# Group size and buffers of the later adaLN products in a two-layer mixer kernel on Trainium2

## The chip, the cores and the metric

The kernel runs on one core of one Trainium2 chip. The metric is device time in microseconds of one execution; before the change the median of three executions is 1592.39 us (1588.01 to 1595.9). The profile shows one further execution, in which the hardware profiler recorded every instruction, every semaphore update and every DMA packet.

## What is computed

Two transformer layers run over 1024 tokens and 256 context tokens of width 1024. Both layers are modulated by a condition vector. This is the part that the change touches:

```python
def adaln_params(cond, w, b):
    m = jax.nn.silu(cond) @ w + b
    return jnp.split(m, 3, axis=-1)          # shift, scale, gate
...
for layer in range(DEPTH):                   # DEPTH = 2
    need_ctx = layer < DEPTH - 1
    shx, scx, gtx = adaln_params(c, adaln_w[layer], adaln_b[layer])
    shc, scc, gtc = adaln_params(c_ctx, adaln_w[layer], adaln_b[layer])
    hx = rms_norm(x, norm_g[layer]) * (1.0 + scx[:, None, :]) + shx[:, None, :]
    hc = rms_norm(ctx, norm_g[layer]) * (1.0 + scc) + shc
    ...                                      # layer 0: attention, layer 1: gated linear attention
    x = x + gtx[:, None, :] * (ox @ w_out[layer])
    if need_ctx:
        ctx = ctx + gtc * (oc @ w_out[layer])
```

`adaln_w` is 2 x 1024 x 3072 in float32. Layer 0's shift and scale are needed at once and are made at the start. Layer 0's gate and all of layer 1's shift, scale and gate are needed later; these are the "later products".

## The kernel before

Layer 0 projects the tokens, six units of weights one after another, and attends: heads of a windowed attention (family A) and of a differential attention (family B, four heads). Function `layer0_heads` runs steps u = 1 to 6. In each step the attention of an earlier unit (`l0_attn_a` or `l0_attn_b`) is written together with fill work for TensorE (`l0_proj`, the projection of unit u, and in step 6 `l0_gates`); `merge` draws the fill in by its costs. In step u = ADP = 4, which has the second family B head and the projection of unit 4, the fill is woven by `weave` with `adaln_later`, a piece for every 2100 units of fill.

`adaln_later` calls `adaln_rows` three times: 256 columns a row group for layer 0's gate, then twice 384 columns for layer 1. One call sums over KB = 8 contraction blocks of 128. For each block it takes two tiles `aw` (128 partitions by 2 x 256 or 2 x 384 columns) from a ring of AWB = 3 buffers, starts their loads on the queue of SyncE (line 238), and issues four matmuls (line 242). The stationary operand is the condition `s32`, 128 x 32; matmul j writes columns 32j to 32j+31 of the array and partitions 32j to 32j+31 of the PSUM tile `AD` (`tile_position`). So there are 3 x 8 x 4 = 96 matmuls and 48 loads. Each matmul is float32 and has two records in the trace. After a call VectorE adds the bias rows `arb` (line 245), and for layer 1 `adaln_cols` transposes the rows and writes `sh1` and `ga1`.

The order within each engine is not the order of the source: when the program is built, a scheduler places each instruction by its own timing and by priority, which follows the source. `ahead(kind)` raises the priority by as many places as AHEAD gives for that kind (`high_priority(offset=n)`). Each engine then runs its list in order; SyncE's queue too is served in order, so a load that waits for a buffer holds up everything behind it.

Names in the rows: `proj` (line 399) are projections, `SX` (1021) the scores of the attention, `T` transposes (`<-ident,p` line 1034, `<-identr,hb` lines 817 and 821), `O` (1046 to 1048, 1064, 1077) the attention's value products and the norms behind them, `h` tiles of normalised tokens loaded from `hT_d`, `wraw` raw weights, `oT_d` the attention's results. The tile pool of the later products, `l0d`, lives in step 4 only.

Of the kernel before, what the change touches and what calls it, by code (L numbers as in the profile page):

```python
# [19 lines left out]
P = 128  # L20
D = 1024
KB = 8
# [44 lines left out]
XP = 2  # L67
NPRE = 0
ADP = 4
AWB = 3  # L70
EPP = 5
RB = 0
PB = 0
AHEAD = dict(gate=100)

ENG = dict(raw="aaaa", vhi="avaa", hb="avaa", qe="avaa", ke="avaa", whi="aaaa", sc="aaaa", pn="pppp", vlo="vppp", wlo="vvvv", hblo="vvvv", sq="aaaa", cos="vvpp", rot="vvpp", xn="vvvv", z="vvvv", x1="vvvv", olo="vvvv")
PSA = dict(T="01", SC="@SX", proj="36", SX="245", O="7")
# [56 lines left out]
class K:  # L134
# [13 lines left out]
    def psum(self, **banks):  # L148

        self.banks = banks  # L150
        self.turn = dict.fromkeys(banks, 0)

    def ahead(self, kind):

        n = AHEAD.get(kind, 0)
        return self.tc.high_priority(offset=n) if n else nullcontext()
# [68 lines left out]
    def adaln_rows(self, layer, c0, n, stage, per, psum, out_pool):  # L225

        nc, a = self.nc, self.a
        ps = psum()
        br = self.st(out_pool, [P, n], "arb")
        for j in range(4):  # L230
            nc.sync.dma_start(br[32 * j:32 * j + 32, :],
                              a["adaln_b"][layer:layer + 1, c0 + n * j:c0 + n * (j + 1)].to_broadcast([32, n]))
        for k in range(KB):
            yield 860 * n / 512
            w = {}
            for j0 in range(0, 4, per):
                t = stage(per * n)
                nc.sync.dma_start(t, a["adaln_w"][layer, k * P:(k + 1) * P, c0 + n * j0:c0 + n * (j0 + per)])
                for j in range(per):
                    w[j0 + j] = t[:, n * j:n * j + n]  # L240
            for j in range(4):
                nc.tensor.matmul(ps[32 * j:32 * j + 32, 0:n], lhsT=self.s32[:, k, :, :].rearrange("p a b -> p (a b)"),  # L242
                                 rhs=w[j], start=(k == 0), stop=(k == KB - 1), tile_position=(0, 32 * j))
        rows = self.st(out_pool, [P, n], "ar")
        nc.vector.tensor_tensor(rows, ps[:, 0:n], br, op=ALU.add)
        return rows
# [41 lines left out]
    def adaln_later(self, pool):  # L288

        nc = self.nc  # L290
        psum = lambda: self.st(self.ps, [P, 512], "AD")
        stage = lambda n: self.st(pool, [P, 384 * APER], "aw", bufs=AWB)[:, 0:n]
        rows = yield from self.adaln_rows(0, 2048, 256, stage, APER, psum, pool)
# [1426 lines left out]
```

## Time and profile before

| | before |
|---|---|
| executions | 1595.9, 1592.39, 1588.01 us; median 1592.39 |
| profiled execution | 1597.08 us, of which its span 1595.3 us |
| TensorE busy | 1482.9 us, 93% of the span |
| VectorE, ScalarE, GpSimd busy | 1017.0, 792.4, 579.6 us (64, 50, 36%) |
| granted TensorE clock, mean | 0.974 |
| line 242, the later products | 96 matmuls, 192 records, between 528.8 and 667.9 us |

A record of a matmul starts when it reads its operands and ends (modelled) when its results are out, so successive ones overlap; the distance between the starts of successive rows is what TensorE spends. The chain of waits is followed back from the last instruction; a wait in it is shown from the start of what was waited for, so a "DMA" piece of the chain is the whole transfer, also where TensorE worked during part of it.

### The profile page before, as it was taken

What the parts mean: (1) busy time and instruction counts of PE and PEld (TensorE: products, weight loads), DVE (VectorE), ACT (ScalarE), POOL (GpSimd) and SP (SyncE); (2) the same over time, 40 slices, a digit from 0 to 9 for tenths busy, and PEclk for the clock granted to TensorE, in tenths of its full rate; (3) what the DMA queues carried; (4) which work ended last, traced back from release to release, by engine and by line L of the source; (5) the groups of instructions that cost most, each with busy time, mean ns of one, the idle gap of its engine ahead of it and who ended that gap; (6) DMA issues with size and microseconds to landing.
All of it is one profiled execution on the core that took longest, in us unless ns stands there. A gap on an engine that the chain in (4) does not pass through costs nothing.

```text
span 1595.3 us, 26832 instructions
## 1 busy us (share of the span) xinstructions
PE 1482.9 (93%) x9460; PEld 1302.5 (82%) x9460; DVE 1017.0 (64%) x2488; ACT 792.4 (50%) x2153; POOL 579.6 (36%) x857
## 2 busy tenths in 40 slices
PE   6897998999899999999999899989989999997998
PEld 4897977888798877688898777878878998896897
DVE  3787678768667666577765767638854536237565
ACT  3665667776756655466645634345642413224111
POOL 1756777988745554247100000001111212112111
PEclk9898999999999999999999999999999999999999
DMA  9732314322231565623323368655673635425542
GB/s 343 301 145 91 120 67 126 126 70 97 83 115 68 175 230 185 199 83 116 104 80 129 123 198 295 249 187 188 231 242 108 237 132 194 166 94 182 168 149 106
DMA packets 108399, 251.30 MB, mean 158 GB/s; under 512 B 10372, under 2 KB 58500, under 8 KB 94440
## 3 DMA queue, kind: packets, MB, share of 16 engines
q1 hardware_dynamic: 108264, 249.58, 46.1%
q8 instruction: 75, 1.23, 0.3%
q14 instruction: 60, 0.49, 0.1%
HBM read 196.78 MB, written 52.76 MB: 156 GB/s over the span
## 4 chain that ended last, share of the span: by engine, by line
PE 65%; DVE 8%; DMA 7%; ACT 4%; issue 3%; POOL 2%; SPq 0%; ACTq 0%; DVEq 0%; POOLq 0%
PE proj L399 40%; PE SX L1021 4%; PE T L1034 2%; PE AD L242 2%; PE S L399 1%; PE O L942 1%; DMA wraw<-in_w_out 1%; DMA wraw<-in_w_head 1%; PE T L931 1%; PE O L1048 1%; PE O L1046 1%; PE O L1047 1%; PE T L1462 1%; ACT p L993 1%; DMA h<-g_d 1%
## 5 line engine op out<-in xcount | busy, mean ns | idle before, releaser
L399 PE MATMUL proj<-w,h 128*128 128x384 f32 (+2 forms) x2544 | 555.2, 359 | 9.1 <-DVE qs L696 3.8
L399 PEld LDWEIGHTS proj<-w,h 128*128 128x128 f32 x2544 | 437.1, 192 | 49.8 <-DVE qs L696 5.4
L399 PE MATMUL proj<-h,w 128*128 128x256 f32 x1800 | 268.3, 291 | 14.0 <-DVE w L412 2.9
L399 PEld LDWEIGHTS proj<-h,w 128*128 128x128 f32 x1800 | 241.3, 194 | 27.4 <-DVE w L412 4.5
L993 ACT ACTIVATE p<-SX,bnm 128x512 f32<-128x512 f32 (+1 forms) x208 | 124.3, 610 | 52.2 <-DVE bnm L986 38.0
L1444 POOL TENSOR_SCALAR Ts<-U,alpha 128x256 f32<-128x256 f32 x64 | 36.9, 577 | 244.4 <-DVE U L1440 244.4
L913 POOL TENSOR_TENSOR wt<-praw,wt 128x512 fp32r<-128x512 f32 (+1 forms) x96 | 114.8, 1209 | 25.5 <-ACT wt L912 20.6
L1021 PE MATMUL SX<-k,q 128*128 128x512 f32 (+1 forms) x416 | 109.0, 371 | 3.4 <-ACT p L993 3.3
L981 DVE TENSOR_REDUCE bnm<-SX 128x1 f32<-128x512 f32 x128 | 86.2, 685 | 39.9 <-PE SX L1021 39.2
L223 POOL TENSOR_TENSOR qr<-qss,mhalf 128x4 f32<-128x4 f32 (+1 forms) x60 | 65.6, 1094 | 67.5 <-DVE qss L769 62.7
L1021 PEld LDWEIGHTS SX<-k,q 128*128 128x128 f32 x416 | 69.0, 190 | 19.8 <-ACT p L993 7.1
L1440 DVE SCALAR_TENSOR_TENSOR U<-U,alpha,S 128x256 f32<-128x256 f32 x64 | 30.6, 478 | 81.4 <-PE S L399 65.1
L787 POOL TENSOR_TENSOR qs<-qs,tab 128x64 f32<-128x64 f32 (+1 forms) x192 | 73.0, 406 | 11.2 <-DVE qs L776 3.3
L223 POOL TENSOR_TENSOR brr<-brs,mhalf 128x2 f32<-128x2 f32 x20 | 16.6, 831 | 164.3 <-DVE brs L1067 145.2
L414 ACT CAST wt<-T 128x512 fp32r<-128x512 f32 (+1 forms) x104 | 50.8, 511 | 43.9 <-PE T L1034 43.6
L415 DVE TENSOR_TENSOR wt<-T,wt 128x512 fp32r<-128x512 f32 (+1 forms) x104 | 59.1, 580 | 13.6 <-ACT wt L414 13.2
L911 ACT COPY praw<-T 128x512 f32<-128x512 f32 (+1 forms) x96 | 49.6, 542 | 34.8 <-PE T L931 34.2
L414 ACT CAST kmt<-T 128x128 fp32r<-128x128 f32 x72 | 18.7, 266 | 95.0 <-PE S L399 48.2
L897 POOL TENSOR_SCALAR p<-p,arz 128x640 f32<-128x640 f32 (+2 forms) x80 | 59.7, 759 | 15.9 <-DVE arz L895 10.4
L223 POOL TENSOR_TENSOR nr<-nms,mhalf 128x1 f32<-128x1 f32 x20 | 11.7, 586 | 146.4 <-DVE nms L339 146.4
L399 PE MATMUL proj<-w,ohl 128*128 128x512 f32 x240 | 62.0, 402 | 2.6 <-DVE ohl L741 1.7
L414 ACT CAST w<-wraw 128x768 fp32r<-128x768 f32 (+2 forms) x48 | 33.7, 727 | 59.9 <-DMA wraw<-in_w_head 37.1
(310 smaller groups left out, 3395.4 us busy)
## 6 DMA issues: line engine op xcount, KB each, us to landing
h<-hT_d SPq DMA_DIRECT2D x50, 1024.0 KB, 5.0
h<-h_d SPq DMA_DIRECT2D x38, 1024.0 KB, 5.0
aw<-in_adaln_w SPq DMA_DIRECT2D x32, 384.0 KB, 3.8
h_d<-h SPq DMA_DIRECT2D x10, 1024.0 KB, 7.3
wraw<-in_w_head SPq DMA_DIRECT2D x24, 384.0 KB, 4.0
xin<-in_x SPq DMA_DIRECT2D x16, 512.0 KB, 5.5
hT_d<-h SPq DMA_DIRECT2D x8, 1024.0 KB, 5.5
g_d<-qs SPq DMA_DIRECT2D x40, 128.0 KB, 1.7
```

Of the source, the lines that this page charges most:

```text
L223: self.nc.gpsimd.tensor_tensor(out, x, self.mhalf[: x.shape[0], : x.shape[1]], op=ALU.pow)
L399: nc.tensor.matmul(ps, lhsT=x, rhs=y, start=(k == 0 and m == 0), stop=(k == n - 1 and m == 2))
L414: self.nc.scalar.copy(hi, src)
L415: self.nc.vector.tensor_tensor(lo, src, f(hi), op=ALU.subtract)
L787: nc.gpsimd.tensor_tensor(m[:, h0:h0 + n, 32 * s:32 * s + 32], xn[:, h0:h0 + n, 32 - 32 * s:64 - 32 * s], sv, op=ALU.mult)
L897: (nc.vector if hh < PN else nc.gpsimd).tensor_scalar(pv[:, hh], pv[:, hh], rz[:, hh:hh + 1], 0.0, op0=ALU.mult, op1=ALU.add)
L911: (nc.vector.tensor_copy if mode == 2 else nc.scalar.copy)(raw, src)
L913: (nc.vector if mode == 4 else nc.gpsimd).tensor_tensor(lo, raw, f(hi), op=ALU.subtract)
L981: nc.vector.tensor_reduce(nmx[:, s, c:c + 1], B, axis=AX.X, op=ALU.max, negate=True)
L993: nc.scalar.activation(pe[s][:, col:col + w], B, AF.Exp, bias=nm, accum_out=Z[:, s, c:c + 1])
L1021: nc.tensor.matmul(out, lhsT=q[:, 2 * x + s, :], rhs=kk[:, s, ks], start=(x == 0), stop=(x == 1))
L1444: nc.gpsimd.tensor_scalar(t, u, self.alpha[:, 4 * d + h, n:n + 1], 0.0, op0=ALU.mult, op1=ALU.add)
```

## The change

The loop over the eight contraction blocks becomes a loop over two groups of ADK = 4. In a group the eight loads come first, with the same cost yielded after each block's two loads, then the group's 16 matmuls, under `ahead("ad")` with an offset of 600. They are written in reverse, last block and last column group first, so that the first matmul of the program order needs the tile that was loaded last; the flags for starting and ending the sum go with the new order. The ring of `aw` has eight buffers, one group's.

```diff
-AWB = 3
+AWB = 8
+ADK = 4
...
-AHEAD = dict(gate=100)
+AHEAD = dict(gate=100, ad=600)
...
-        for k in range(KB):
-            yield 860 * n / 512
+        for k0 in range(0, KB, ADK):
             w = {}
-            for j0 in range(0, 4, per):
-                t = stage(per * n)
-                nc.sync.dma_start(t, a["adaln_w"][layer, k * P:(k + 1) * P, c0 + n * j0:c0 + n * (j0 + per)])
-                for j in range(per):
-                    w[j0 + j] = t[:, n * j:n * j + n]
-            for j in range(4):
-                nc.tensor.matmul(ps[32 * j:32 * j + 32, 0:n], lhsT=self.s32[:, k, :, :].rearrange("p a b -> p (a b)"),
-                                 rhs=w[j], start=(k == 0), stop=(k == KB - 1), tile_position=(0, 32 * j))
+            for k in range(k0, k0 + ADK):
+                for j0 in range(0, 4, per):
+                    t = stage(per * n)
+                    nc.sync.dma_start(t, a["adaln_w"][layer, k * P:(k + 1) * P, c0 + n * j0:c0 + n * (j0 + per)])
+                    for j in range(per):
+                        w[k, j0 + j] = t[:, n * j:n * j + n]
+                yield 860 * n / 512
+            with self.ahead("ad"):
+                for k in reversed(range(k0, k0 + ADK)):
+                    for j in reversed(range(4)):
+                        nc.tensor.matmul(ps[32 * j:32 * j + 32, 0:n],
+                                         lhsT=self.s32[:, k, :, :].rearrange("p a b -> p (a b)"), rhs=w[k, j],
+                                         start=(k == ADK - 1), stop=(k == KB - ADK), tile_position=(0, 32 * j))
```

Line 242 of before is line 246 after, and line 238 is 239; other lines behind the change move by five. In the rows of the program's order below, x2 stands for two matmuls in a row of the same operands' tiles; the numbers behind the names tell buffers apart.

TensorE's list where the later products begin, before (`AD` from line 242, two matmuls for each tile `aw`):

```order
L1021 MATMUL SX_7380<-k_5635,q_6360 128x256 x2
L242 MATMUL AD_7352<-aw_7422,s_17_124 32x256 x2
L242 MATMUL AD_7352<-aw_7424,s_17_124 32x256 x2
L242 MATMUL AD_7352<-aw_7461,s_17_124 32x256 x2
L1034 MATMUL T_7051<-ident_61,p_6735 128x128 x2
L399 MATMUL proj_7335<-w_7318,h_6511 128x384
L1021 MATMUL SX_7438<-k_5635,q_6360 128x256 x2
L399 MATMUL proj_7335<-w_7318,h_6511 128x384 x2
L399 MATMUL proj_7335<-w_7323,h_6511 128x384
L1046 MATMUL O_7095<-wt_1573_6897,v_3843 128x256
L1047 MATMUL O_7095<-wt_1573_6897,v_3843 128x256
L242 MATMUL AD_7352<-aw_7463,s_17_124 32x256 x2
```

The same place after:

```order
L1026 MATMUL SX_7384<-k_5635,q_6360 128x256 x2
L246 MATMUL AD_7352<-aw_7545,s_17_124 32x256 x2
L246 MATMUL AD_7352<-aw_7543,s_17_124 32x256 x2
L246 MATMUL AD_7352<-aw_7463,s_17_124 32x256 x2
L246 MATMUL AD_7352<-aw_7461,s_17_124 32x256 x2
L246 MATMUL AD_7352<-aw_7428,s_17_124 32x256 x2
L246 MATMUL AD_7352<-aw_7426,s_17_124 32x256 x2
L246 MATMUL AD_7352<-aw_7360,s_17_124 32x256 x2
L246 MATMUL AD_7352<-aw_7358,s_17_124 32x256 x2
L1039 MATMUL T_7051<-ident_61,p_6735 128x128 x2
L404 MATMUL proj_7335<-w_7318,h_6511 128x384
L1026 MATMUL SX_7438<-k_5635,q_6360 128x256 x2
```

A whole group stands in one piece, at the place where six matmuls stood. The second group follows 22 rows behind the first.

TensorE's fourth group after, the one with a foreign row in it (the fifth has two projections in it, behind its first two matmuls):

```order
L246 MATMUL AD_7874<-aw_8380,s_17_124 32x384 x2
L246 MATMUL AD_7874<-aw_8378,s_17_124 32x384 x2
L246 MATMUL AD_7874<-aw_8339,s_17_124 32x384 x2
L246 MATMUL AD_7874<-aw_8337,s_17_124 32x384
L1069 MATMUL O_7589<-ones_68,sc_7616 128x1 x2
L246 MATMUL AD_7874<-aw_8337,s_17_124 32x384
L246 MATMUL AD_7874<-aw_8251,s_17_124 32x384 x2
```

Here 7 and 9 matmuls stand on the two sides of a small product; of the six groups four are unbroken.

SyncE's queue at one place before, where loads of `aw`, of tokens `h` and stores of results alternate:

```order
L1081 DMA oT_d_87<-sc_7612 128x256
L358 DMA h_7835<-hT_d_80 128x2048
L238 DMA aw_8196<-in_adaln_w 128x768
L358 DMA h_8114<-hT_d_81 128x2048
L238 DMA aw_8198<-in_adaln_w 128x768
L238 DMA aw_8245<-in_adaln_w 128x768
```

SyncE's queue after, ahead of the sixth group:

```order
L1086 DMA oT_d_87<-sc_7612 128x256
L363 DMA h_7831<-hT_d_80 128x2048
L363 DMA h_8110<-hT_d_81 128x2048
L239 DMA aw_8787<-in_adaln_w 128x768
L239 DMA aw_8789<-in_adaln_w 128x768
L239 DMA aw_8791<-in_adaln_w 128x768
L239 DMA aw_8793<-in_adaln_w 128x768
L239 DMA aw_8800<-in_adaln_w 128x768
```

The eight loads of a group (five of them shown) now stand together, behind a store and two loads of `h`. The loads of the first group stand further back in the queue than the first three did (row 151 instead of 82), still far ahead of step 4.

## Rows read from the trace of the kernel before

**Rows 1.** The page: busy time by engine, chain by engine and by line.

```profile
PE 1482.9 (93%) x9460; PEld 1302.5 (82%) x9460; DVE 1017.0 (64%) x2488; ACT 792.4 (50%) x2153; POOL 579.6 (36%) x857
...
PE 65%; DVE 8%; DMA 7%; ACT 4%; issue 3%; POOL 2%; SPq 0%; ACTq 0%; DVEq 0%; POOLq 0%
```

**Rows 2.** Chain of waits, 525 to 680 us: shares, pieces (start us, us, what).

```profile
by line: PE proj L399 32.6%; PE AD L242 18.7%; PE SX L1021 14.2%; PE T L1034 7.1%; DMA aw<-in_adaln_w 5.4%; PE O L1048 4.2%; PE O L1046 3.8%; PE O L1047 3.7%; PE T L817 2.1%; PE O L1077 1.6%; PE O L1064 1.3%; PE T L821 1.1%; ACT p L993 1.0%
...
528.38 0.47 PE SX L1021 x4
...
546.86 0.44 PE T L1034 x4
...
551.57 0.92 PE SX L1021 x4
...
571.51 3.13 PE proj L399 x18
...
612.17 0.47 PE T L817 x4
...
628.91 0.34 PE O L1064 x4
```

**Rows 3.** Stretches: busy us (x) of PE, PEld, DVE, ACT, POOL; clock, DMA, GB/s.

```profile
10.00:34.00 24.00, 19.92 (x281) 13.26 (x274) 10.35 (x30) 8.41 (x18) 0.88 (x1) 1.00 1.05 400
...
528.00:668.00 140.00, 136.26 (x865) 101.49 (x863) 84.19 (x222) 75.42 (x221) 62.43 (x109) 0.99 0.61 201
```

**Rows 4.** The same columns, neighbouring stretches and the one with waits.

```profile
760.00:800.00 40.00, 36.45 (x264) 33.97 (x263) 30.30 (x75) 23.03 (x66) 5.94 (x11) 0.96 0.28 97
...
640.00:660.00 20.00, 17.24 (x99) 10.64 (x99) 9.29 (x19) 9.31 (x28) 6.68 (x12) 0.91 0.77 238
697.00:815.00 118.00, 111.76 (x772) 104.70 (x771) 86.09 (x222) 73.97 (x220) 48.14 (x79) 0.99 0.31 105
```

**Rows 5.** Line 242 alone, 515 to 680 us: busy PE and PEld, clock, DMA.

```profile
515.00:680.00 165.00, 32.76 (x192) 6.64 (x192) 0.99 0.58 191
```

**Rows 6.** TensorE in order of time: start us, us, line, form, records [idle before <-releaser].

```profile
528.78 1.06 PE L242 MATMUL AD<-aw,s 128*32 128x256 f32 x12
529.77 0.44 PE L1034 MATMUL T<-ident,p 128*128 128x128 f32 x2
...
532.38 0.63 PE L242 MATMUL AD<-aw,s 128*32 128x256 f32 x4 [0.97 <-DMA aw<-in_adaln_w]
532.93 0.51 PE L1021 MATMUL SX<-k,q 128*128 128x256 f32 x2
...
537.65 0.66 PE L1034 MATMUL T<-ident,p 128*128 128x128 f32 x4
538.23 0.63 PE L242 MATMUL AD<-aw,s 128*32 128x256 f32 x4
538.79 0.66 PE L1034 MATMUL T<-ident,p 128*128 128x128 f32 x4
539.20 0.71 PE L1021 MATMUL SX<-k,q 128*128 128x512 f32 x2
```

**Rows 7.** The same view, products with 384 columns.

```profile
577.81 1.48 PE L242 MATMUL AD<-aw,s 128*32 128x384 f32 x12
579.23 0.49 PE L1077 MATMUL O<-sc,ones 128*128 128x128 f32 x2
...
589.07 0.85 PE L242 MATMUL AD<-aw,s 128*32 128x384 f32 x8
589.85 0.39 PE L1046 MATMUL O<-wt,v 128*128 128x256 f32 x1
...
592.83 0.83 PE L242 MATMUL AD<-aw,s 128*32 128x384 f32 x2
593.59 0.44 PE L1034 MATMUL T<-ident,p 128*128 128x128 f32 x2
```

**Rows 8.** The same view, the two waits behind 645 us and what follows them.

```profile
647.55 0.84 PE L242 MATMUL AD<-aw,s 128*32 128x384 f32 x4 [1.17 <-DMA aw<-in_adaln_w]
...
651.22 1.48 PE L242 MATMUL AD<-aw,s 128*32 128x384 f32 x4 [1.60 <-DMA aw<-in_adaln_w]
652.62 1.11 PE L1034 MATMUL T<-ident,p 128*128 128x128 f32 x4
653.39 0.99 PE L399 MATMUL proj<-w,h 128*128 128x384 f32 x2
```

**Rows 9.** DMA issues: tiles, queue, count, KB each, median us to landing.

```profile
h<-hT_d SPq DMA_DIRECT2D x50, 1024.0 KB, 5.0
...
aw<-in_adaln_w SPq DMA_DIRECT2D x32, 384.0 KB, 3.8
...
aw<-in_adaln_w SPq DMA_DIRECT2D x16, 256.0 KB, 2.9
```

**Rows 10.** Line 238, all its loads: landing; SyncE's waits (total us, times, longest).

```profile
DMA to landing us min/median/max: 2.6/3.6/8.4
...
SPq L358 <- PE proj L399: 280.2, 68, 15.5
```

**Rows 11.** SyncE in order of time: three stores that end the heads of family B.

```profile
565.49 0.33 SPq L1081 DMA_DIRECT2D oT_d<-sc  x1
...
677.64 19.17 SPq L1081 DMA_DIRECT2D oT_d<-sc  x2
...
815.11 0.38 SPq L1081 DMA_DIRECT2D oT_d<-sc  x1
```

**Rows 12.** Chain of waits behind step 4: the transfers in it.

```profile
753.90 2.62 DMA wraw<-in_w_gate
...
812.82 6.21 DMA h<-hT_d
```

## The prediction

> **What bounds the kernel now.** I read the page first, for which engine sets the time. TensorE is busy for 93% of the span and makes 65% of the chain of waits; no other engine has over 8% of it [rows 1]. So what the change gives must come off TensorE, and in one stretch only, the fourth step of layer 0, where line 242 runs. The chain of that stretch is the second view: the later products are 18.7% of its 155 us, 29.0 us, and transfers of their weights another 5.4% [rows 2]. The third is the table of stretches: between 528 and 668 us TensorE is busy for 136.26 of 140 us while VectorE, ScalarE and GpSimd have 84, 75 and 62 us [rows 3]. A microsecond taken off TensorE there is therefore at first worth a microsecond; the question is what comes up behind it.
>
> **What the products cost now.** Line 242 has 192 records in 32.76 us of busy time [rows 5], in 39 separate rows of TensorE's list in order of time, of which rows 6 and 7 show five and rows 8 two. Read the distances between starts. With 256 columns, 4 records (two matmuls) hold TensorE for 532.93 - 532.38 = 0.55 us, and 12 records (six matmuls) for 0.99 us [rows 6]. With 384 columns, 2 records (a single matmul) cost 0.76 us, 8 records (four) 0.78 us, and 12 records 1.42 us [rows 7]. So one matmul costs as much as four: those on four different column groups run beside each other, as one round, and a round that holds one or two wastes the rest. A further round in the same piece adds 0.99 - 0.57 = 0.42 us (0.57 being my value for a first round with 256 columns, from 0.55) or 1.42 - 0.78 = 0.64 us. The busy time of a row reaches some 0.07 us into the next one (0.63 against 0.55), so the 39 rows hold TensorE for about 32.76 - 39 x 0.07 = 30.0 us.
>
> **What they cost in groups.** Sixteen matmuls in one piece are four rounds: 0.57 + 3 x 0.42 = 1.83 us, or 0.78 + 3 x 0.64 = 2.70 us. Two groups of the first and four of the second width make 14.5 us. The fourth and fifth group are broken once each, into 7 + 9 and 2 + 14; each break costs a round more at a first round's price, 0.78 us. That is 16.0 us: **14.0 us less**. Then the way into a piece: four transposes ahead of line 242 take 538.23 - 537.65 = 0.58 us, the same four ahead of a score product 539.20 - 538.79 = 0.41 us [rows 6]. I take 0.1 us for each entry (bounds 0 and 0.17); 8 pieces instead of 39 save **3.1 us** (0 to 5.3).
>
> **Waits of before that go.** TensorE stood for 0.97, 1.17 and 1.60 us on loads of `aw` [rows 6, 8], **3.7 us**: a load could start only when one of three buffers came free. Behind the last of these waits the granted clock fell to 0.91 in the mean of 640 to 660 us [rows 4], a few microseconds at the lower of its two levels: a round took 652.62 - 651.22 = 1.40 instead of 0.77 us, four transposes 0.77 instead of 0.41 us [rows 8, 6]. That is **1.0 us** more.
>
> **Waits that come.** The ring holds one group, so the next group's eight loads start when a burst has ended, and the next burst needs the last of them at once. TensorE's list is in order: everything behind the burst, projections, scores and transposes, waits with it. The first group has its loads long before. For the others I set the work that stands between two bursts against the loading. Prices of the work, from starts: a projection 3.13 / 18 = 0.174 us, a score product 0.23 (512 columns) or 0.12 (256), a transpose 0.11, the other kind 0.12, a product of ones 0.17 [rows 2], a value product 0.12, which I set equal to the 256-column score. Between the first and second burst stand 9 projections, 10 + 6 transposes, 2 + 4 scores, 6 value products and 2 of ones: 1.57 + 1.82 + 0.94 + 0.72 + 0.34 = 5.4 us. The same count gives 15.6, 10.4, 13.2 and 12.0 us for the four later gaps (43, 29, 48 and 24 projections among them). Loading: in the prologue, all loads back to back, the core moved 400 GB/s [rows 3], which is 0.66 us for 256 KB, 0.98 us for 384 KB, 2.6 us for a 1 MB tile `h`. With the median landing of the first, 2.9 or 3.8 us [rows 9], eight take 2.9 + 7 x 0.66 = 7.5 us (8.0 us with a `wraw` among them) or 3.8 + 7 x 0.98 = 10.7 us, and 13.3 us where an `h` is ahead. The waits are then 8.0 - 5.4 = 2.6, 0, 0.3, 0.1 and 13.3 - 12.0 = 1.3 us: **4.3 us lost**. Bounds: 0, if other engines hold up the work between the bursts and the loads get their time; and, with the longest landing seen, 8.4 us [rows 10], 8.1 + 0 + 4.9 + 2.1 + 3.3 = 18.4 us. I take 4.3, nearer to the medians. One of them, the 2.6 us, is longer than the one that brought the clock down, so **1.0 us** goes for that (0 to 4).
>
> **Idle time that comes up.** In the next step, with the same attention and projections and no later products, TensorE is busy for 111.76 of 118 us, idle for 5.3% [rows 4]; in step 4 it is never idle for another engine, because the products fill the holes. Some 100 us of other work stay there (136.26 - 32.76, less the entries). At 5.3% that is 5.3 us; where the bursts and waits let the others catch up, nothing. About 43 us of the work come behind the last burst and have no filler. I take **4.0 us** lost (0 to 8.9, the latter at the 8.9% of 760 to 800 us).
>
> **At no cost.** VectorE's bias sums, the column copies, the bias loads and the stores of the rows keep their number; they read results that come earlier than before. The first eight loads move back in SyncE's queue, past stores and two loads of `h`, to a place still far ahead of 528 us. The larger pool delays the reload of layer 0's gate rows in the queue; they are used two steps later. The scheduler's order behind step 4 shifts too; from the transfers in the chain there, 2.62 and 6.21 us long [rows 12], I allow 4 us either way.
>
> **Sum**, against the profiled execution: 14.0 + 3.1 + 3.7 + 1.0 - 4.3 - 1.0 - 4.0 = 12.5 us less than 1597.1, which is 1584.6 us. That execution lies 4.7 us above the median of the three, 1592.4; against the median the forecast is **1580 us**.
>
> **Rivals.** First, the gain is taken up by the pace of the other engines. The head's end is stored at 565.49, 677.64 + 19.17 = 696.81 and 815.11 us [rows 11]: step 4 takes 131.3 us, the next one 118.3 us. If everything but TensorE needs those 118.3 us, no more than 13 us can be had, and with TensorE idle at the 8.9% of the worst neighbour and the order behind it 1.5 us worse, 12.5 - 4.9 - 1.5 = 6 us are left: 1586 us, within what counts as no change. For it speaks that the neighbours do idle; against it that VectorE, the busiest of the others, has 73% there.
>
> Second, slower: SyncE's queue holds the loads up. Groups 3 to 6 have loads behind loads of `h`, and those wait for TensorE to leave a buffer: 280.2 us over 68 waits, 4.1 in the mean, 15.5 at most [rows 10]. If each of the four groups starts loading 6 us late, the waits are 2.6 + 3.7 + 6.3 + 6.1 + 7.3 = 26 us with 5 us at the lower clock, and 17.1 + 4.7 - 26 - 5 - 4 = -13: 1605 us. It decides from about 13 us of waiting on. Against it: before, the loads of the same `h` tiles stood ahead of loads of `aw` too, and most of these buffers come free ahead of the burst.
>
> Third, the clock. What is seen: behind the wait of 1.60 us a round ran at 1.40 us, not 0.77 [rows 8]. If every one of the five later bursts ran so, they would cost their 1.83 + 4 x 2.70 = 12.6 us again, and the time would stay at 1592 us. The Trainium skill's page "TensorE: Matmul & The Clock Gate" (Loop structure matters more than you think) names just this pattern as bad, a wait for a DMA between bursts of matmuls, after which they run cold; the trace agrees at 651 us and not at 532 us, where a wait of 0.97 us was followed by rounds at full price. Against the rival: between the bursts TensorE has 5 to 16 us of other work, and only one or two waits are as long as that.
>
> That the change doesn't do what it says can be left aside: the list of each engine is fixed, and four of six groups stand in one piece.
>
> **How the numbers follow.** 0.60 for the forecast, 0.24 for the pace of the others (1586), 0.08 for the clock (1592), 0.08 for the queue (1605). Half a per cent, 8 us, is about what a measurement tells from no change: faster 0.60, same 0.32, slower 0.08. The range runs from 1570, with the new waits and the idle time near 0 and the entries at their upper bound, to 1594, past the clock's case; it leaves out the queue's and about as much below.
>
> **What would show it.** In the profile after, line 246 should be busy for some 16 to 17 us in 8 rows, four of them with 32 records at 1.8 or 2.7 us; a wait of 2 to 4 us on `aw` ahead of the second burst, under 2 us ahead of the others; step 4, by the same stores, some 12 us shorter, the steps behind as long as before. TensorE idle for 8% or more behind the last burst would be the first rival, waits of 6 us with stalled `h` loads the second, bursts of 3.5 us and more the third. The forecast is wrong if the step gets shorter but the end does not follow.

## The result and the profile after

The changed kernel takes 1578.72 us in the median of four executions (1574.15 to 1580.66), the kernel before 1592.93 us in the median of four (1588.01 to 1595.9). The ratio is 0.9901, with a 95% interval of 0.9876 to 0.9926: 14.2 us less, where 1580 us was forecast. The profiled execution took 1577.39 us, 19.7 us less than the profiled one of before; that this difference is larger than the one of the medians comes up again below.

The page of the changed kernel: span, TensorE's busy time, and the chain by engine (compare [rows 1]).

```profile
span 1575.7 us, 26816 instructions
...
PE 1471.4 (93%) x9460; PEld 1304.4 (83%) x9460; DVE 1015.9 (64%) x2488; ACT 793.1 (50%) x2153; POOL 581.5 (37%) x857
...
PE 62%; DVE 11%; DMA 6%; ACT 4%; issue 3%; POOL 2%; SPq 0%; DVEq 0%; ACTq 0%; POOLq 0%
```

TensorE lost 11.5 us of busy time with the same number of instructions; the other engines' work is unchanged to 2 us. VectorE's share of the chain of waits rose from 8 to 11%, and TensorE's fell from 65 to 62%.

The later products, line 246, between 515 and 680 us (busy us of PE and PEld, clock, DMA; compare [rows 5]):

```profile
515.00:680.00 165.00, 17.94 (x192) 6.25 (x192) 0.97 0.52 182
```

The same 192 records are busy for 17.94 us, not 32.76. In TensorE's order of time (start us, us, line, form, records, [idle before <-releaser]) they are eight rows, of which these are the first seven, with what stands around the first two:

```profile
522.90 1.93 PE L246 MATMUL AD<-aw,s 128*32 128x256 f32 x32
524.77 0.44 PE L1039 MATMUL T<-ident,p 128*128 128x128 f32 x2
...
531.42 0.45 PE L404 MATMUL proj<-w,h 128*128 128x384 f32 x1 [1.73 <-ACT w L164]
...
533.58 3.20 PE L246 MATMUL AD<-aw,s 128*32 128x256 f32 x32
536.71 0.62 PE L404 MATMUL proj<-w,h 128*128 128x384 f32 x2
...
552.53 2.79 PE L246 MATMUL AD<-aw,s 128*32 128x384 f32 x32
...
565.90 1.49 PE L246 MATMUL AD<-aw,s 128*32 128x384 f32 x14
567.33 0.61 PE L1069 MATMUL O<-ones,sc 128*128 128x1 f32 x4
567.86 2.12 PE L246 MATMUL AD<-aw,s 128*32 128x384 f32 x18
...
583.10 0.84 PE L246 MATMUL AD<-aw,s 128*32 128x384 f32 x4
...
584.50 2.77 PE L246 MATMUL AD<-aw,s 128*32 128x384 f32 x28
```

The first burst holds TensorE for 524.77 - 522.90 = 1.87 us, the price of four rounds that the prediction gave (1.83). Three things are new. The products are over at 602 us, where before they reached 668. There is one wait of note, 1.73 us, and it isn't ahead of a burst: a projection waits for ScalarE to write a `w`, a tile of converted weights. And the second burst, 2.2 us behind that wait, takes 536.71 - 533.58 = 3.13 us where the first took 1.87; these are matmuls at the lower of the clock's two levels, 1.2 GHz, as behind the wait in [rows 8].

The table of stretches, with the columns of [rows 3]: the few microseconds around the second burst, the products' stretch, and step 4 behind the last burst.

```profile
523.00:537.00 14.00, 11.91 (x107) 8.10 (x108) 8.11 (x24) 6.06 (x18) 5.70 (x9) 0.88 0.68 214
...
523.00:602.00 79.00, 76.79 (x585) 61.66 (x585) 46.15 (x126) 42.19 (x124) 36.35 (x65) 0.98 0.79 286
602.00:682.00 80.00, 74.45 (x464) 67.02 (x461) 60.60 (x167) 51.55 (x153) 44.05 (x80) 0.96 0.25 86
```

Around the second burst the granted clock is 0.88 in the mean. In the products' stretch TensorE is idle for 2.2 us (3.7 before, [rows 3]), and behind the last burst for 5.6 of 80 us. What it waits for there, the three longest (engine, line, waited for: us, times, longest):

```profile
PE SX L1026 <- ACT p L998: 2.2, 4, 1.6
PE T L1039 <- DVE bzs L1005: 1.4, 1, 1.4
PE proj L404 <- ACT w L164: 0.8, 1, 0.8
```

The first two are the attention's own waits, for ScalarE's and VectorE's part of the softmax: the idle time that the prediction expected once no products stand in those holes. Part of it was there before: in the 29 us between the last product and the end of step 4, before, TensorE was idle for 3.1 us.

Last, the stores that end the heads of family B on SyncE's queue (compare [rows 11]):

```profile
558.97 0.33 SPq L1086 DMA_DIRECT2D oT_d<-sc  x1
...
682.00 0.32 SPq L1086 DMA_DIRECT2D oT_d<-sc  x1
...
796.19 0.32 SPq L1086 DMA_DIRECT2D oT_d<-sc  x1
```

Step 4 takes 123.0 us from start to start, the next one 114.2 us. Before, it was 131.0 and 118.6 us by the same starts (696.50 us is the start of the second store in the row that begins at 677.64; the prediction's 131.3 and 118.3 go by the end of that row). The two together are 12.4 us shorter.

### The profile page after: what moved, and what is told of

Its sections match the earlier page's. It is cut to its first block, busy times and chain, and to the rows that moved or that the text cites. A ratio compares the mean times of both kernels' runs of the same rounds, so it can differ in the third digit from the quotient of the medians.

```text
span 1575.7 us, 26816 instructions
## 1 busy us (share of the span) xinstructions
PE 1471.4 (93%) x9460; PEld 1304.4 (83%) x9460; DVE 1015.9 (64%) x2488; ACT 793.1 (50%) x2153; POOL 581.5 (37%) x857
## 4 chain that ended last, share of the span: by engine, by line
PE 62%; DVE 11%; DMA 6%; ACT 4%; issue 3%; POOL 2%; SPq 0%; DVEq 0%; ACTq 0%; POOLq 0%
PE proj L404 40%; PE SX L1026 4%; PE T L1039 2%; DMA wraw<-in_w_out 1%; PE S L404 1%; DMA h<-g_d 1%; PE O L947 1%; PE T L936 1%; ACT p L998 1%; PE AD L246 1%; DMA D<-D_d 1%; DVE bnm L986 1%; PE O L1053 1%; PE O L1052 1%; PE O L1051 1%
```

## The experiments

The theory on trial: TensorE pays for a round whether one or four matmuls are in it, and the gain comes from whole rounds. The rivals: the gain comes from the eight buffers (loads earlier, no waits on `aw`); from the longer groups; or from the products being done earlier. "Busy" below is line 246's (242's) busy time between 500 and 700 us, "hold" the sum of the distances from each of its rows to the next row, "to the end of layer 0" the time from the first product to the start of the last record of layer 0's output projection. Within that time, "idle" is TensorE's idle time, and "at 1.2 GHz" the time for which its other work, all but the products, ran at the lower of the two granted clocks. Pieces are counted in the program's order of TensorE. Ratios are to the kernel before on the same chip.

| kernel | pieces | busy us | hold us | idle us | at 1.2 GHz, us | to the end of layer 0, us | median us | ratio (95%) |
|---|---|---|---|---|---|---|---|---|
| before | 39 | 32.76 | 30.0 | 26.5 | 15.1 | 508.2 | 1592.93 | |
| before_again | 39 | 32.78 | 30.0 | 25.2 | 15.3 | 506.6 | 1594.9 (one) | |
| changed | 8 | 17.94 | 17.4 | 22.8 | 21.6 | 493.5 | 1578.72 | 0.9901 (0.9876 to 0.9926) |
| changed_again | 8 | 17.61 | 17.1 | 26.0 | 15.5 | 494.3 | 1581.88 | 0.9929 (0.9907 to 0.9951) |
| forward_order | 36 | 32.48 | 30.0 | 26.3 | 6.5 | 508.2 | 1599.25 | 1.0052 (1.0026 to 1.0079) |
| ring_of_eight | 29 | 26.57 | 24.5 | 25.2 | 23.9 | 505.7 | 1591.17 | 1.0003 (0.9983 to 1.0022) |
| no_priority | 21 | 22.25 | 20.8 | 21.6 | 12.6 | 491.8 | 1581.86 | 0.9927 (0.9902 to 0.9953) |
| groups_of_one | 19 | 17.72 | 16.4 | 23.1 | 10.2 | 488.7 | 1578.51 | 0.9922 (0.9898 to 0.9946) |
| groups_of_two | 16 | 18.33 | 17.2 | 24.9 | 10.1 | 489.7 | 1576.47 | 0.989 (0.9864 to 0.9916) |
| quarter_products | 6 | 5.93 | 5.5 | 24.0 | 16.4 | 479.1 | 1571.7 | 0.9867 (0.9826 to 0.9909) |
| before_wraw3 | 37 | 33.58 | 31.3 | 23.4 | 19.9 | 506.4 | 1587.08 | 0.996 (0.9938 to 0.9983) |
| changed_wraw3 | 7 | 15.85 | 15.4 | 27.4 | 18.7 | 492.4 | 1577.88 | 0.9903 (0.9865 to 0.994) |
| one_wraw3 | 19 | 17.72 | 16.4 | 27.5 | 27.1 | 499.1 | 1579.66 | 0.991 (0.9878 to 0.9942) |

The two added columns close the account. A record at the lower clock takes about twice its time (1.40 for 0.77 us in [rows 8]), so half of the time at 1.2 GHz is lost. Take the hold, the idle time and that half off the stretch, and 440 to 444 us are left in every kernel but forward_order, where it is 448.8. So the hold is one of three things that move the time, and a change of it shows in the time only as far as the other two stand still. How much of the clock belongs to a kernel and how much to an execution, two profiles can't tell: 15.1 and 15.3 us for the kernel before, 21.6 and 15.5 for the changed one. The mean granted clock of all executions says something of it: 0.974 over the 41 of the kernel before, 0.972 over ten of ring_of_eight, 0.971 over eight of the changed kernel, 0.978 over ten of before_wraw3. Among those 41 of one kernel, each further microsecond of clock not granted (one less the clock, times the span) goes with 0.67 us of time (correlation 0.75).

**The order of writing alone.** Buffers, groups and priority stay; only the matmuls of a group are written first block first.

```diff
-                for k in reversed(range(k0, k0 + ADK)):
-                    for j in reversed(range(4)):
+                for k in range(k0, k0 + ADK):
+                    for j in range(4):
...
-                                         start=(k == ADK - 1), stop=(k == KB - ADK), tile_position=(0, 32 * j))
+                                         start=(k == 0), stop=(k == KB - 1), tile_position=(0, 32 * j))
```

> The changed kernel with the 16 matmuls of a group written forward (first block and first column group first) instead of reversed; ring of eight and priority 600 stay. In the built order the products then stand in 36 pieces with 42 rounds of up to four, against 39 pieces and 42 rounds before and 8 pieces with 26 rounds in the changed kernel. Theory P (the gain is packing: fewer rounds and entries on TensorE): the products hold TensorE for some 30 us again, and only the old waits on loads are gone: 1587 to 1592 us. Theory B (the gain is the ring of eight, loads long ahead of use): 1578 to 1582 us, like the changed kernel. Theory E (the 6 us by which the changed kernel is ahead when the products begin, 522.9 against 528.8 us, come from its first loads standing further back in SyncE's queue): the products begin at 523 us here too.

The products alone between 500 and 700 us, and the stretches with products, behind them in step 4, and the next step:

```profile
500.00:700.00 200.00, 32.48 (x192) 6.84 (x192) 1.00 0.45 158
...
527.00:611.00 84.00, 83.29 (x520) 52.66 (x519) 40.93 (x110) 35.00 (x104) 29.94 (x51) 1.00 0.72 256
611.00:698.00 87.00, 79.66 (x508) 70.93 (x505) 61.90 (x171) 54.98 (x162) 48.03 (x91) 1.00 0.27 89
```

With all of the change but the order, the price is the old one, 32.48 us, and the kernel is 0.5% slower than before, slower than either theory had it. The waits on `aw` are nearly gone (TensorE is idle for 0.7 us where the products are), and nothing is won by that: behind them it is idle for 7.3 of 87 us. Products done early are no gain. Of the 0.5% a part can be placed: TensorE's other work, the same 2783 records, takes 4.7 us more than before at full clock (448.8 against 444.1 us), in small amounts on projections, transposes and value products, which stand in another order. In the profiled execution less time at the lower clock hides it; over all executions the mean clock is the same as before's, 0.974. Why that order costs more is open.

**The buffers alone.** The kernel before with a larger ring.

```diff
-AWB = 3
+AWB = 8
```

> The kernel before with AWB = 8 alone; loop, order and priority as before. Built order: 29 pieces, 36 rounds, by the prices of the prediction 24.8 us and 2.9 us of entries, against 30.0 and 3.9 before. Theory P: 6 us from packing and some 4 us from waits that go, less 2 us of idle time: 1584 to 1588 us. Theory B: 1578 to 1582 us. Theory E: the products begin at 523 us instead of 529.

The products, step 4 behind them, and the next step:

```profile
500.00:700.00 200.00, 26.57 (x192) 6.01 (x192) 0.97 0.47 168
...
614.00:689.00 75.00, 70.44 (x433) 64.43 (x434) 57.41 (x159) 45.87 (x136) 38.38 (x74) 0.93 0.26 89
689.00:811.00 122.00, 112.45 (x760) 105.50 (x759) 84.03 (x215) 73.67 (x218) 49.62 (x85) 0.96 0.29 99
```

What TensorE waited for between 615 and 815 us:

```profile
PE proj L399 <- ACT qs L163: 4.7, 3, 1.8
PE SX L1021 <- ACT p L993: 4.0, 4, 1.3
```

Free buffers let the scheduler put more matmuls together (29 pieces), 5.5 us come off the hold, and 1.0003 comes out, where 1584 to 1588 us was expected from packing. Of the 5.5 us 2.5 are left at the end of layer 0 (508.2 against 505.7 us). The next step has TensorE idle for 9.6 of 122 us, against 6.2 of 118 in [rows 4]. Over the whole stretch idle time is no longer than before; what takes the gain back in this execution is the clock, 0.93 and 0.96 in the last two rows against 0.99 in [rows 4]: 8.8 us more of the other work run at 1.2 GHz, which is 4.4 us. Larger buffers alone give nothing that can be measured in the time.

**Shorter groups.** First `ADK = 4` to `1`, then to `2`, all else as changed.

> The changed kernel with ADK = 1: groups of one contraction block (4 matmuls, one round), ring of eight, priority 600, so loads may run three blocks ahead. Built order: 19 pieces, 24 rounds, 16.3 us and 1.9 us of entries against 16.0 and 0.8 in the changed kernel. Theory P: packing within a round is all that counts and nearly everything of it is here; the wait of a whole group for its last load is not, so 1575 to 1580 us, equal to the changed kernel or up to 3 us better. If long unbroken groups are what counts (entries dear), 1584 us or more.

> The changed kernel with ADK = 2: groups of two blocks, so that the ring of eight holds two groups and the next one loads while one is multiplied. Built order: 16 pieces, 26 rounds, 17.1 us and 1.6 us of entries. Theory P: as groups of one and four, 1576 to 1581 us. If the double buffer is worth something by itself, under 1576 us.

Groups of one, in TensorE's order of time: the last four blocks of the first row group (256 columns) and the first block of the second (384):

```profile
529.30 0.64 PE L246 MATMUL AD<-aw,s 128*32 128x256 f32 x8 [0.92 <-DMA aw<-in_adaln_w]
531.76 0.64 PE L246 MATMUL AD<-aw,s 128*32 128x256 f32 x8
534.18 0.64 PE L246 MATMUL AD<-aw,s 128*32 128x256 f32 x8
536.36 0.64 PE L246 MATMUL AD<-aw,s 128*32 128x256 f32 x8
541.64 0.85 PE L246 MATMUL AD<-aw,s 128*32 128x384 f32 x8
```

Each of these rows is a round of four matmuls (8 records) at its first-round price. Of the 19 pieces 16 are like that; the other three have 16, 8 and 8 matmuls. Together they hold TensorE for 16.4 us, no more than the 17.4 of the changed kernel's eight pieces. So a group needs to be one block only: what counts is that its four column groups stay together. Sixteen in a piece save a little in each further round, and in the changed kernel that is given back at the second burst. Groups of two are the fastest complete version that was run, 1576.47 us, but its interval and those of the other two lie over each other.

**The priority.**

```diff
-AHEAD = dict(gate=100, ad=600)
+AHEAD = dict(gate=100)
```

> The changed kernel without the raised priority of the later products (no entry for ad); groups of four, reversed order and ring of eight stay. Built order: 21 pieces, 31 rounds, 20.8 us and 2.1 us of entries on TensorE, against 16.8 together in the changed kernel and 33.9 before. Theory P: the time lies between the two in that proportion, some 4 to 6 us above the changed kernel: 1582 to 1586 us. If only whole unbroken groups give the gain (as the runs with 29 and 36 pieces could mean, which gave nothing), it is near before: 1588 to 1592 us.

```profile
500.00:700.00 200.00, 22.25 (x192) 5.66 (x192) 0.97 0.48 169
```

Without it the groups fall into 21 pieces, with 4.3 us more busy time and 3.4 us more hold than changed, and the time is no different, where 4 to 6 us more were expected: 0.9927 here, 0.9929 for the changed kernel on the same chip. In the profiled executions the longer hold is made up for by less idle time and less time at 1.2 GHz (the table). The reversed order, with groups and eight buffers, carries the change; that the priority adds something, the runs don't show.

**A quarter of the products.** Of each group only the last block is multiplied (`for k in (k0 + ADK - 1,)`), so three quarters of the products are left out; all loads stay.

> The changed kernel with three of every four matmuls of the later products left out (a group multiplies its last contraction block alone; all loads stay), so the modulation of layer 1 and the gate of layer 0 are incomplete. Built order: 6 pieces, 8 rounds, 5.5 us and 0.6 us of entries, 10.7 us less on TensorE than in the changed kernel. If step 4 is still bound by TensorE after the change, the time falls by about 8 to 11 us, to 1568 to 1571 us. If the other engines have become the pace (first rival of the prediction), it falls by under 4 us: 1575 to 1579 us. Buffers that nobody reads come free at once, so waits on loads may be shorter too; that is in both.

```profile
500.00:700.00 200.00, 5.93 (x48) 1.41 (x48) 1.00 0.39 136
...
526.00:565.00 39.00, 37.38 (x253) 30.11 (x252) 25.01 (x68) 21.59 (x66) 20.61 (x36) 1.00 0.80 282
565.00:682.00 117.00, 109.44 (x716) 100.42 (x715) 89.26 (x247) 76.84 (x229) 63.58 (x114) 1.00 0.29 102
```

The hold falls by another 17.4 - 5.5 = 11.9 us, and the time by 7 to 10 us (from 1578.72, and from 1581.88, the changed kernel's median in the repetition below), or 5 to 10 by the ratios, whose intervals reach 4 to 7 us to either side: between the two expectations, nearer to the first. In the profiled executions layer 0 is shorter by all of it, 14 to 15 us, and TensorE is no longer idle there than in the changed kernel (24.0 us, against 22.8 and 26.0); what is missing lies behind layer 0 (562.8 us to the end, against 559.2 and 558.9). So after the change the step is still TensorE's, and the pace of the others, the first rival, isn't seen in it. Set beside forward_order, the time falls by 27.6 us for 24.5 us of hold; the 4.7 us of forward_order's longer other work are in that.

**The new wait.** In the changed kernel the projection that waits 1.73 us needs the last piece of unit 4's weights. SyncE's queue there (start us, us, line, tiles, count):

```profile
511.94 8.02 SPq L589 DMA_DIRECT2D wraw<-in_w_unit  x5
523.57 3.04 SPq L239 DMA_DIRECT2D aw<-in_adaln_w  x4
526.70 0.38 SPq L589 DMA_DIRECT2D wraw<-in_w_unit  x1
527.13 1.84 SPq L239 DMA_DIRECT2D aw<-in_adaln_w  x4
```

The load of `wraw` stands behind four loads of the second group, which themselves waited for the first burst to free the ring. It lands 4.13 us later, as the chain of waits of that stretch has it, ScalarE converts it, and TensorE goes on:

```profile
526.70 4.13 DMA wraw<-in_w_unit
530.86 0.52 ACT w L164
```

If this is the cause, a third buffer for `wraw` (`"wraw", bufs=2` to `bufs=3`, in three places) lets all its loads start ahead of the group. It was tried in the changed kernel, in the kernel before, and with groups of one.

> The changed kernel with three buffers instead of two for the raw weights wraw. In the built queue of SyncE all loads of unit 4's weights then stand ahead of the second group's loads, while in the changed kernel the last one stands behind four of them and TensorE waits 1.73 us for it, with the second burst at half the clock behind it (3.13 instead of 1.83 us). Theory Q (the wait that the change brings sits in SyncE's queue, not at the burst): from the start of the first burst to the end of the second 11 to 12 us instead of 13.8, the second burst at 1.8 to 1.9 us, 2 to 4 us off the whole: 1574 to 1577 us. If the loads of the group itself are the limit, the second burst waits some 2 us on aw and the time stays at 1578 to 1580 us.

> The kernel before with three buffers for wraw: what the third buffer gives by itself, in the weights of all steps and of the output products. Built order: 37 pieces, 43 rounds, so the products cost as before. Theory Q: within 3 us of before, 1589 to 1593 us. If the raw weights' buffers are what counts in general, under 1587 us.

> Groups of one block (ADK = 1), ring of eight, priority 600, and three buffers for wraw. Built order: 19 pieces, 24 rounds. Groups of one had no wait of a whole group, but its loads shared the queue with wraw too. Theory P with Q: 1573 to 1578 us, the best of all by 1 to 3 us. If the small groups gain nothing from the third buffer: 1577 to 1580 us.

SyncE's queue of changed_wraw3, and TensorE's two first bursts:

```profile
506.91 8.55 SPq L589 DMA_DIRECT2D wraw<-in_w_unit  x7
519.61 4.02 SPq L239 DMA_DIRECT2D aw<-in_adaln_w  x8
```

```profile
518.95 1.93 PE L246 MATMUL AD<-aw,s 128*32 128x256 f32 x32
...
529.68 1.93 PE L246 MATMUL AD<-aw,s 128*32 128x256 f32 x32
531.55 0.87 PE L1039 MATMUL T<-ident,p 128*128 128x128 f32 x6
```

Seven loads of `wraw` in a row come first, the wait is gone, and the second burst takes 531.55 - 529.68 = 1.87 us. The hold is 15.4 us; this order has one break less than the changed kernel, so by the prediction's prices it is 16.0 - 0.78 = 15.2. With the wait the second burst ran at the lower clock in both profiles of the changed kernel, without it at the full one: that is the 1.3 us that the hold is over its forecast. The time doesn't follow: 1577.88 us, no better than changed and outside the 1574 to 1577 of theory Q, and with groups of one the third buffer gives nothing either. In the kernel before it is worth 0.4%, more than expected. The profiles say where that arises: with three buffers the later products begin at 519 to 521 us in all three kernels (523 to 529 us in the others). Ahead of them TensorE is idle between its records for 38 us, not 42 to 46, and at the lower clock for 30.7 us, not 34 to 48. In the profiled execution of changed_wraw3 this is given back behind layer 0: 566.4 us to the end, of which 31.8 idle, against 559.2 and 558.9 us for the changed kernel with 23.1 and 23.7 idle. One profile doesn't tell whether every execution is so.

**Once more.** The kernel before was profiled a second time, and the changed one profiled and timed a second time.

> The kernel before, once more, for a second profile. Theory E: the products begin at 528 to 530 us again, since the queue's order makes them late. If the 6 us are chance from one execution to the next, another start, anywhere from 522 to 530 us.

> The changed kernel once more, for a second profile and more times. 1577 to 1581 us. If the lead of 5.9 us at the start of the products (522.9 against 528.8 us) belongs to the kernel, the products begin at 522 to 524 us again; if most of it is chance, at 525 to 528 us, as in the two runs with the same order up to there (526.8 and 527.0 us).

```profile
528.01 1.93 PE L246 MATMUL AD<-aw,s 128*32 128x256 f32 x32
...
536.76 0.44 PE L404 MATMUL proj<-w,h 128*128 128x384 f32 x1 [1.90 <-ACT w L164]
...
539.22 2.87 PE L246 MATMUL AD<-aw,s 128*32 128x256 f32 x32
542.02 0.61 PE L404 MATMUL proj<-w,h 128*128 128x384 f32 x2
```

The changed kernel comes out at 1581.88 us here, ratio 0.9929 (0.9907 to 0.9951). The wait is again there, with 1.90 us, and the second burst behind it takes 542.02 - 539.22 = 2.80 us. In this execution the products start at 528.0 us, as in the kernel before (528.8 in both of its profiles), and not at 522.9. So of the 19.7 us between the first two profiles some 5 to 6 lie ahead of step 4 and are chance of the execution. Most of it is the clock: ahead of the products TensorE spent 34.1 us at 1.2 GHz in that execution, 41.0 us in this one and 44.4 us in both of the kernel before. What repeats is the stretch from the first product to the end of layer 0, 508.2 and 506.6 us before, 493.5 and 494.3 us after: 12 to 15 us, which is what the medians show (11.8 and 14.2 us).

## Why the prediction was right, point by point

- **TensorE bounds the step.** Right: with the hold unchanged nothing is gained (forward_order), with 12.6 us less of it the time falls by 12 to 14 us (changed), with 11.9 us less again by another 5 to 10 (quarter_products). It isn't a microsecond for each microsecond: idle time and clock move too, and in ring_of_eight they took a gain of 5.5 us back.
- **A round costs the same with one matmul as with four.** Right, and it is the cause of the gain: with the rounds whole, line 246 fell to 17.94 us, and with every other part of the change but the order it stayed at 32.48, without a gain in time.
- **Hold 30.0 to 16.0, 14.0 us less.** It measured 17.4, so 12.6 us less. The prices were right (1.87 for 1.83 us, and 2.72 for 2.70). The missing 1.3 us are the second burst, 3.13 instead of 1.87 us. The prediction had this loss, as a 1.0 us term of its own; it is counted once.
- **Entries, 3.1 us.** The price was right: in the kernel before, where neither a wait nor the lower clock is in it, the last record ahead of a piece takes longer to the next start than the same record ahead of other work: a projection 0.26 to 0.27 us in all eleven cases instead of 0.175, a score product of 512 columns 0.32 to 0.33 in ten instead of 0.23. That is 0.09 us for each of 31 entries saved, 2.8 us. It doesn't show as such in the sum: what is left of the stretch without hold, idle time and clock fell by 0.2 to 1.5 us only, since the other work stands in another order too.
- **Waits of before, 3.7 us, and of after, 4.3 us.** The waits of before went; but forward_order, where nearly all waits on `aw` are gone too, gained nothing. What was wrong is the **place** of the new wait: 2.6 us were forecast ahead of the second burst, on `aw`, from the work between two bursts set against the loading. The trace has no wait on `aw` there, and 1.73 us at a projection 2 us earlier. The only wait on `aw` is ahead of the fourth group, where TensorE is idle for 0.12 us (0.72 in the repetition). The count had the `wraw` load in it ("8.0 us with a `wraw` among them") as a load that delays the group; it is the group that delays the load, which other work needs sooner. In all TensorE is idle for 2.2 us in the products' stretch, so the new waits were less than forecast by half.
- **The clock at the new wait, 1.0 us.** Right in burst and near in size (1.3 us in the first profile, 0.9 in the second), though the wait ahead of it was another one. The clock elsewhere has no term in the forecast, and it counts as much: up to 6.5 us more of the other work at 1.2 GHz, 3.2 us of time, in the first profile, 0.1 us in the second. That all five later bursts run so, the third rival, is refuted: the third row of 32 records is busy for 2.79 us and holds TensorE for 2.72, the price at 2.4 GHz.
- **Idle time that comes up, 4.0 us.** 5.6 us behind the last burst (7.0% of 80 us), inside the bounds of 0 to 8.9. But TensorE was idle for 3.1 us of the 29 us behind the last product before, so that step 4 was not without such waits. With the waits on loads in it, the idle time from the first product to the end of step 4 went from 6.9 to 7.8 us. The stretch was sized at 43 us of work; it is 80 us long, because the products move to the front of the step (they end at 602 us, not 668; with the buffers alone at 614, in no_priority at 618).
- **Step 4 some 12 us shorter, the next as long as before.** Wrong in the split, right in the sum: 8.0 and 4.4 us. The scheduler moved work between the steps: between the same stores the next step has 734 records of TensorE, 776 before.
- **The other rivals.** The pace of the others: 7.0% idle, under the 8% that would have been its sign, and quarter_products has no more idle time in layer 0. SyncE's queue held nothing up by 6 us; its main effect is the 1.73 us.

The mechanism was right, and that the sum came so near is in part luck. From the first product to the end of layer 0 the two pairs of profiles give: hold 12.6 and 13.0 us less (14.0 forecast); idle time 3.7 us less and 0.8 us more (4.6 us more forecast, all waits together); the lower clock in the other work 3.2 and 0.1 us more (nothing forecast but the two terms of 1.0 us, which cancel); the rest 1.5 and 0.2 us less (3.1 us for the entries). In all it is 14.6 and 12.3 us less, against a sum of 12.5. Waits that were forecast too dear made up for a hold, entries and a clock that were forecast too well.

## What to carry to other kernels

Count TensorE's work in column-tiled matmuls by rounds, not by matmuls: read the distance between starts, and see whether the four column groups stand side by side in the engine's list. To keep them together, let the first of them in the program's order be the one whose operand comes last (reversed order); more buffers alone don't do it. Read idle time and granted clock over the same stretch before you call a gain missing, or credit one. Where a group's loads start in one go on an in-order queue, look for what other work's load stands in the middle of them, and expect a stretch without its filler to show the other engines' waits.

## What the runs showed of the hardware that was not expected

- A single matmul of 128 x 32 on 128 x 384 holds TensorE for 0.76 us and four on four column groups for 0.78 us [rows 7]; in a longer piece each further round of four costs 0.64 us. The Trainium skill's page "TensorE: Matmul & The Clock Gate" (Part 3: Packing small matmuls) describes packed tiles as running beside each other at a few nanoseconds for each further one. The trace agrees, with 0.02 us for three further ones; a piece with one tile alone pays nearly the whole, 0.76 us.
- The wait behind which the clock falls can belong to other work than the matmuls that pay for it: 1.73 us at a projection, and the burst that starts 2.2 us later runs at 1.2 GHz (3.13 us for 1.87; 2.80 in the repetition, behind 1.90 us), while a wait of 0.92 us right ahead of a round in groups_of_one was followed by a round at full price (0.64 us, as the others).
- Two profiled executions of the same program can differ by 5 us in when step 4 starts (522.9 and 528.0 us), with no change in the program, and the time at the lower clock ahead of it differed by 7 us (34.1 and 41.0). A stretch measured from its own first instruction repeated to 1 to 2 us (493.5 and 494.3; 508.2 and 506.6).
- Between executions of one kernel the mean granted clock varies (0.970 to 0.979 over 41 of the kernel before) and the time goes with it, 0.67 us for each microsecond of clock not granted.
